# Two places of a form arena filled one block earlier, and its two tiles cut at another form

## The chip, the cores and the metric

The kernel runs on one core of one Trainium2 chip. The metric is the device time of one execution in microseconds (us); lower is better. Times of a kernel are given as the median of several executions. One further execution of each kernel is recorded by the hardware profiler; all rows shown below come from such a profiled execution.

## The reference

One encoder block on x of shape (1, 512, 2048), all in float32: a norm and a combined input projection, two attention mixers, an output projection with a residual, a gated feed-forward network with a residual, and a final norm. The change touches how the feed-forward part's operands are laid out and brought in:

```python
x = x + jnp.einsum('bse,ed->bsd', mixed, w_out[layer])
h2 = rmsnorm(x, g_ffn[layer])
gate, up = jnp.split(jnp.einsum('bsd,df->bsf', h2, w_gate_up[layer]), 2, axis=-1)
x = x + jnp.einsum('bsf,fd->bsd', jax.nn.silu(gate) * up, w_down[layer])
return rmsnorm(x, g_final)
```

Here d = 2048 and f = 5632, so w_down is (5632, 2048): 44 row chunks of 128, taken in 22 pairs.

## The kernel before, in words

**Arithmetic.** Each float32 operand is split in a high part, which ScalarE (ACT) rounds to TensorE's own format, and a low part, which VectorE (DVE) makes by subtraction. A product is three matmuls (`mm3`, lines 231 to 233): high by high, high by low, low by high.

**Seven forms.** Large products go by a scheme of Strassen's kind: for each pair of row chunks, the left operand (activations) is turned into seven *forms* (`m1` to `m7`), sums and differences of its quarters, and so is the weight side. Seven products replace eight.

**The arena.** The left forms lie in an SBUF arena with 7 forms by 8 pairs by (high, low) by 256 columns. It consists of two tiles: `arena[0]` with the first `EARLY` = 3 forms of `ORDER`, `arena[1]` with the other 4. `form_tile(m, pairs)` finds a place by form and pair. The same memory serves other data in earlier stages (`WA_HOMES`, `O_HOMES`, `place`).

**Head.** While the first projection runs, `x_prep(k)` transposes chunk k of x on TensorE, ACT copies it out and makes its high parts (line 327), DVE its low parts (line 328). When both chunks of a pair are there, `x_sums` makes the sums (lines of `form_sums`, 349), and `x_split` splits them: two ACT instructions (line 344) and two DVE instructions (line 345) a pair, each for two neighbouring forms.

**The down projection.** The gate and up blocks write the forms of their result to DRAM (`forms_dram`). The down product runs over its 22 pairs in three groups, `DOWN_PAIRS = (6, 8, 8)`, since the arena holds 8 pairs. Every group is two column blocks (`down_block`, 1024 output columns each), called here block (group, column block). A block goes through the forms in the order `CHAIN` = m1, m7, m6, m2, m5, m4, m3 (with m5 moved in front of most of m2), a unit for each form and pair: 42 units in a block of group 0, 56 in the others. A unit is one weight form split into `tw` (ACT line 755, DVE line 758), for four of the seven forms after a DVE sum or difference of raw weights (line 795), and six matmuls. ACT and DVE prepare a unit some 8 us of planned time ahead.

**Queues.** Raw weights are loaded by SP's queue (`Raw.load`, line 260) 20 us of planned time ahead, as tiles come free. What the blocks add up is evicted by ACT (line 1133) and added into DRAM by POOL's queue (line 1134).

**The next group's forms.** `next_forms(box, first, pairs)` brings the forms of the next group into the arena while the last block of the group before runs, and on into the group's own first block. Each form comes in pieces of up to 4 pairs. A piece is three steps: a load on ACT's DMA queue into one of two `fr` tiles (line 1107), the high part on ACT (line 1110), the low part on DVE (line 1113). The steps hang on unit numbers (`hook`): the form's last unit plus 4 for each form before it, plus 4 for the second piece, and then -5, +1 and +3 for the three steps. Group 0 fills only places 0 to 5 of every form; group 1 fills all 8 places, as two pieces of 4 pairs a form.

**Order of the work.** A loop over all units issues, for each unit in turn, the loads, the splits ahead, the unit's matmuls and then its hooks. Every engine goes through its own instructions in that order, so an instruction that waits holds back all that follow on its engine, the DMA issues on ACT included.

Of the kernel before, what the change touches and what calls it, by code (L numbers as in the profile page):

```python
# [11 lines left out]
F32 = mybir.dt.float32  # L12
BF16 = mybir.dt.bfloat16
F32R = mybir.dt.float32r
AF = mybir.ActivationFunctionType
OP = mybir.AluOpType
# [3 lines left out]
P = 128  # L20
# [4 lines left out]
KD = D // P  # L25
# [25 lines left out]
RAWS = {"raw": 6, "craw": 24, "craw0": 24, "kraw": 9, "craw40": 18, "draw6": 21, "draw8": 28}  # L51
W_TILES = {"wi": 10, "wo": 12}
DOWN_PAIRS = (6, 8, 8)
ORDER = ("m1", "m7", "m6", "m2", "m4", "m5", "m3")
EARLY = 3
EVICT = 6
HEAD_RATE = (1.42, 1.9)
TURN_LAG = 6
# [5 lines left out]
def f32(ap):  # L64
    return ap.bitcast(F32)
# [3 lines left out]
def encoder_block(ctx, tc, x, g_mix, w_in, g_q_a, g_k_a, g_out_a, g_out_b, w_out, g_ffn,  # L69
# [75 lines left out]

    def form_tile(m, pairs):
        return arena[0][:, m, pairs] if m < EARLY else arena[1][:, m - EARLY, pairs]

    def place(m, i):
        return form_tile(m, i).rearrange("p a b -> p (a b)")  # L150
# [78 lines left out]
    def mm3(dst, a, b, start, stop, chained=False):  # L229
        (ah, al), (bh, bl) = a, b  # L230
        nc.tensor.matmul(dst, ah, bh, start=start, stop=False, skip_group_check=chained)  # L231
        nc.tensor.matmul(dst, ah, bl, start=False, stop=False, skip_group_check=chained)  # L232
        nc.tensor.matmul(dst, al, bh, start=False, stop=stop, skip_group_check=chained)  # L233

    def cols(pair, lo, n=P):
        return pair[0][:, lo:lo + n], pair[1][:, lo:lo + n]
# [4 lines left out]
    def in_turn(tiles, n, shape, dtype, tag):  # L241
        if not tiles and homing[0]:
            whole = sp.tile([P, n] + shape[1:], dtype, tag=tag + "s", bufs=1, name=nm(tag))
            tiles.extend(whole[:, i] for i in range(n))
        if not tiles:
            tiles.extend(sp.tile(shape, dtype, tag=tag, bufs=n, name=nm(tag)) for _ in range(n))
        tiles.append(tiles.pop(0))
        return tiles[-1]

    class Raw:  # L250
        def __init__(self, pieces, first=0, tag="raw", width=2 * 512):
            self.pieces, self.first, self.tag, self.width, self.t = pieces, first, tag, width, None
# [11 lines left out]
    class Unit:  # L264
# [22 lines left out]
        def split_lo(self):  # L287
            nc.vector.tensor_tensor(self.w[1], self.src, f32(self.w[0]), op=OP.subtract)  # L288
# [7 lines left out]
    def hook(n, f):  # L296
        hooks.setdefault(n, []).append(f)
# [11 lines left out]
    def x_prep(k):  # L309
        ps = bank()  # L310
        for t in range(NT):
            nc.tensor.transpose(ps[:, t * P:(t + 1) * P], xs[k][:, t, :], ident)
        i, half = divmod(k, 2)
        if half == 0:
            xpair[i] = in_turn(pairs_turn, 3, [P, 4 * 512], F32, "xpair")
        flat = xpair[i][:, half * 1024:half * 1024 + 512]
        view = flat.rearrange("p (f c) -> p f c", c=256)
        hi, lo = (arena[half][:, 0:2, i, j] for j in range(2))
        gain = gm[:, k:k + 1]
        if k == 0:  # L320
            ps3 = ps.rearrange("p (f c) -> p f c", c=256)
            nc.scalar.activation(hi, ps3, AF.Copy, scale=gain)
            nc.vector.scalar_tensor_tensor(lo, ps3, gain, f32(hi), op0=OP.mult, op1=OP.subtract)
            nc.scalar.activation(flat, ps, AF.Copy, scale=gain)
        else:
            nc.scalar.activation(flat, ps, AF.Copy, scale=gain)
            nc.scalar.activation(hi, view, AF.Copy)
            nc.vector.tensor_tensor(lo, view, f32(hi), op=OP.subtract)  # L328
        release(ps)
        row_squares(k)  # L330
        if half == 0:
            hook(k, lambda: nc.gpsimd.dma_start(ar_dram[:, i], arena[0][:, 1, i]))
        else:
            hook(k + 2, lambda: x_sums(i))
            hook(k + 3, lambda: x_split(i))
# [4 lines left out]

    def x_split(i):
        parts = xpair[i].rearrange("p (f c) -> p f c", c=256)
        for src, dst in ((parts[:, 2:4], arena[0][:, 1:3, i]), (parts[:, 6:8], arena[1][:, 2:4, i])):
            nc.scalar.activation(dst[:, :, 0], src, AF.Copy)
            nc.vector.tensor_tensor(dst[:, :, 1], src, f32(dst[:, :, 0]), op=OP.subtract)

    def form_sums(a_l, a_r, b_l, b_r, s1, s2, s3, s4):
        def tt(out, x, y, op=OP.subtract):
# [377 lines left out]
    def form_of(form, i):  # L726
        t = form_tile(ORDER.index(form), i)
        return t[:, 0], t[:, 1]
# [32 lines left out]
            self.box.multiply(self)  # L761

    class ColBlock:
        def __init__(self, w, row, lo, pairs, plan, tag, ready=None, close=None, chain=CHAIN, apart=False):
            self.pairs, self.plan, self.ready, self.close = pairs, plan, ready, close
            self.banks = dict(CHAIN_BANK, m3="x") if apart else CHAIN_BANK
            self.last_of_bank = LAST_OF_BANK + ("m5",) if apart else LAST_OF_BANK
            self.opening = ("m1", "m7", "m2") + (("m3",) if apart else ())
            self.ps, self.at, self.held = {}, {}, []

            def raw(i, j, q):
                at = row + (2 * q + i) * P
                return Raw(lambda t: [(w[0, at:at + P, lo[j]:lo[j] + 512], t)], tag=tag, width=512)
            kinds = {"a": (0, 0), "b": (0, 1), "c": (1, 1), "d": (1, 0), "e": (0, 1), "f": (1, 0), "g": (1, 1)}
            self.raws = [{n: raw(i, j, q) for n, (i, j) in kinds.items()} for q in range(pairs)]
            order = [(form, q) for form in chain for q in range(pairs)]
            if ready is not None:
                rest = order[6:8] + order[8:3 * pairs] + order[3 * pairs + 6:]
                order = order[:6] + order[3 * pairs:3 * pairs + 6] + rest
            if plan is KEPT:  # L780
                at = 3 * pairs + 2
                order[at:at + 2 * pairs - 2] = order[at + pairs - 2:at + 2 * pairs - 2] + order[at:at + pairs - 2]
            for form, q in order:
                self.at[form] = len(units)
                src, dst = plan[form]
                need = src + (dst,) if dst not in src else src
                units.append(Cols(self, form, q, [self.raws[q][n] for n in need]))
                if close is not None and form == CHAIN[-1]:
                    units[-1].dur = COLS_US / 2
# [14 lines left out]
        def multiply(self, u):  # L804
            dst, i = self.bank_of(u.form), u.i
            if self.ready is not None:
                drain_until(lambda: self.ready[i])
            ending = self.close is not None and u.form == "m3"
            if ending:
                self.held.append(u)  # L810
            for t in range(1 if ending else 2):
                mm3(dst[t], cols(form_of(u.form, i), t * P), (u.pair[:, 0], u.pair[:, 1]),
                    u.form in self.opening and i == 0, i == self.pairs - 1, True)
            if ending and i == self.pairs - 1:
                self.close(self)
# [276 lines left out]
    def load_x1(c, rows):  # L1092
        for t in rows:
            x1.setdefault((c, t), slot("x1"))
            nc.gpsimd.dma_start(x1[c, t], x1_dram[c, t])

    def next_forms(box, first, pairs):
        seq = sorted(CHAIN, key=box.at.get)

        def ready(form, h):  # L1100
            m, st = ORDER.index(form), {}
            lo_q, n = 4 * h, min(4, pairs - 4 * h)
            hi, lo = (form_tile(m, slice(lo_q, lo_q + n))[:, :, j] for j in range(2))

            def load():
                st["t"] = in_turn(frs, 2, [P, 4, 256], F32, "fr")[:, :n]
                nc.scalar.dma_start(st["t"], forms_dram[:, m, first + lo_q:first + lo_q + n])  # L1107

            def split_hi():
                nc.scalar.activation(hi, st["t"], AF.Copy)  # L1110

            def split_lo():
                nc.vector.tensor_tensor(lo, st["t"], f32(hi), op=OP.subtract)  # L1113
            late = 4 * seq.index(form) + 4 * h
            box.after(form, late - 5, load)
            box.after(form, late + 1, split_hi)
            box.after(form, late + 3, split_lo)
        for form in seq:
            for h in range(-(-pairs // 4)):
                ready(form, h)  # L1120

    gfin = []
    fin = {}
    def down_block(first, pairs, cb, last):
        box = ColBlock(w_down, 2 * first * P, (cb * 1024, cb * 1024 + 512), pairs, KEPT, f"draw{pairs}",
                       close=finish if last else None)

        def add(form, i, j):
            def go():
# [92 lines left out]
        write_rows(1, 2)  # L1222

    first = 0
    for n in DOWN_PAIRS:
        next_forms(box, first, n)
        for cb in range(2):
            box = down_block(first, n, cb, (first + n, cb) == (NFF // 2, 1))
        first += n

    at = [0.0]
# [135 lines left out]
```

## Time and profile before

| what | value |
|---|---|
| median of 3 runs | 2020.4 us (2019.68 to 2021.6) |
| profiled execution, its own time | 2024.38 us |
| its span in the profile | 2022.6 us |
| TensorE matmuls (PE) busy | 1989.3 us, 98% |
| DVE busy | 1572.3 us, 78% |
| ACT busy | 1113.3 us, 55% |
| moved by DMA | 390.61 MB |

A group's row has the line, the engine, the operation, written and read tiles with their shapes, the count, then busy us and mean ns of one. A row of waits has who waited, for whom, then us in total, times, and the longest. A row of a stretch has its bounds, its length, then each engine's busy us with its count of instructions in brackets, the granted clock of TensorE (PEclk, 1.00 is full speed), the share of the DMA engines, and GB/s.

### The profile page before, as it was taken

To read this page: it belongs to the slowest core of one execution; us is meant where nothing else is said; L and a number is where in the kernel's file an instruction comes from. 1 tells how busy PE (TensorE), PEld (TensorE's weight loads), DVE (VectorE), ACT (ScalarE), POOL (GpSimd) and SP (SyncE) were. 2 spreads that over 40 slices of the span, in tenths; PEclk is the share of its full clock that TensorE was granted. 3 is DMA by queue.
4 is the path that set the end of the run, shared out by engine and by line. 5 is a ranking of instruction groups with operands and counts; after the bars stand their busy time and mean duration, and the time that the engine had idled before them with its cause. 6 is when DMAs were issued, how large, how long until landed. Compare 5 with 4: busy or idle time off the path is not lost. (4 is left out here: it accounts for less than half of the span.)

```text
span 2022.6 us, 27400 instructions
## 1 busy us (share of the span) xinstructions
PE 1989.3 (98%) x9019; PEld 1633.7 (81%) x9019; DVE 1572.3 (78%) x2773; ACT 1113.3 (55%) x1964; POOL 149.9 (7%) x172
## 2 busy tenths in 40 slices
PE   9999999999999999999999999999999999999997
PEld 6788887887788888888888888888888887788886
DVE  7988866576754688878877878878779986887876
ACT  7655345555543565555555555555556665666655
POOL 4100100000010000000000000000000121111122
PEclk9999999999999999999999999999999999999999
DMA  8576533335244545737647657558458798768854
GB/s 267 188 261 228 177 115 103 110 115 171 89 147 140 205 145 198 260 128 259 237 140 273 210 173 273 175 185 287 149 203 280 194 243 256 196 168 261 224 113 178
DMA packets 231391, 390.61 MB, mean 193 GB/s; under 512 B 21408, under 2 KB 70352, under 8 KB 231120
## 3 DMA queue, kind: packets, MB, share of 16 engines
q1 hardware_dynamic: 204880, 326.13, 48.0%
q0 software_dynamic: 14960, 33.04, 8.0%
q10 hardware_dynamic: 11408, 29.70, 4.2%
q8 instruction: 70, 1.15, 0.2%
q14 instruction: 73, 0.60, 0.1%
HBM read 325.08 MB, written 63.70 MB: 192 GB/s over the span
## 5 line engine op out<-in xcount | busy, mean ns | idle before, releaser
L231 PE MATMUL b<-tw,arena 128*128 128x512 f32 x2136 | 838.8, 393 | 4.3 <-ACT ev L1133 2.2
L232 PE MATMUL b<-tw,arena 128*128 128x512 f32 x2136 | 834.4, 391 | 4.2 <-DVE tw L758 3.2
L233 PE MATMUL b<-tw,arena 128*128 128x512 f32 x2136 | 834.1, 390 | 3.4 <-DVE arena L328 3.4
L755 ACT ACTIVATE tw<-raw 128x512 fp32r<-128x512 f32 x924 | 559.5, 628 | 443.7 <-DVE raw L795 286.0
L758 DVE TENSOR_TENSOR tw<-raw,tw 128x512 fp32r<-128x512 f32 x924 | 618.1, 685 | 174.2 <-ACT tw L755 172.1
L232 PEld LDWEIGHTS b<-tw,arena 128*128 128x128 f32 x2136 | 402.1, 188 | 90.5 <-DVE tw L758 7.6
L233 PEld LDWEIGHTS b<-tw,arena 128*128 128x128 f32 x2136 | 401.9, 188 | 89.4 <-DVE arena L328 5.7
L231 PEld LDWEIGHTS b<-tw,arena 128*128 128x128 f32 x2136 | 402.1, 188 | 87.2 <-ACT ev L1133 2.9
L795 DVE TENSOR_TENSOR raw<-raw,raw 128x512 f32<-128x512 f32 x528 | 360.6, 683 | 0.9 <-DMA raw<-in_w_gate_up_dram 0.6
L1134 POOL DMA_DIRECT2D x1d<-ev x76 | 66.5, 978 | 1158.5 <-ACT ev L1133 1157.0
L231 PE MATMUL b<-w,arena 128*128 128x512 f32 x368 | 146.1, 397 | 0.0
L233 PE MATMUL b<-w,arena 128*128 128x512 f32 x368 | 143.8, 391 | 0.0
L232 PE MATMUL b<-w,arena 128*128 128x512 f32 x368 | 143.4, 390 | 0.0
L233 PEld LDWEIGHTS b<-w,arena 128*128 128x128 f32 x368 | 69.1, 188 | 15.0
L232 PEld LDWEIGHTS b<-w,arena 128*128 128x128 f32 x368 | 69.2, 188 | 13.8
L231 PEld LDWEIGHTS b<-w,arena 128*128 128x128 f32 x368 | 69.1, 188 | 13.6
L755 ACT ACTIVATE tw<-stage 128x512 fp32r<-128x512 f32 x90 | 54.5, 628 | 42.2 <-DVE stage L795 33.2
L223 DVE TENSOR_TENSOR pTl<-b,pTh 128x512 fp32r<-128x512 f32 x64 | 44.0, 687 | 34.9 <-ACT pTh L222 24.1
L288 DVE TENSOR_TENSOR w<-raw,w 128x512 fp32r<-128x512 f32 x96 | 64.7, 684 | 5.6 <-ACT w L283 3.2
L349 DVE TENSOR_TENSOR pair<-pair 128x256 f32<-128x256 f32 x120 | 45.5, 420 | 27.3 <-ACT pair L990 26.2
L1133 ACT ACTIVATE ev<-b,smalls 128x512 f32<-128x512 f32 x76 | 49.7, 683 | 26.4 <-PE b L233 25.1
L1037 DVE TENSOR_TENSOR s<-b,s 128x512 f32<-128x512 f32 x66 | 44.0, 687 | 24.8 <-PE b L233 24.8
(197 smaller groups left out, 1808.1 us busy)
## 6 DMA issues: line engine op xcount, KB each, us to landing
raw<-in_w_gate_up_dram SPq DMA_DIRECT2D x616, 256.0 KB, 5.3
raw<-in_w_down_dram SPq DMA_DIRECT2D x176, 256.0 KB, 7.0
stage<-in_w_in_dram SPq DMA_DIRECT2D x106, 256.0 KB, 4.8
forms<-pair SPq DMA_DIRECT2D x22, 896.0 KB, 5.3
x1d<-ev POOLq DMA_DIRECT2D x76, 256.0 KB, 6.6
fr<-forms ACTq DMA_DIRECT2D x35, 512.0 KB, 5.8
raw<-in_w_in_dram SPq DMA_DIRECT2D x64, 256.0 KB, 4.5
raw<-in_w_out_dram SPq DMA_DIRECT2D x32, 512.0 KB, 4.7
```

The lines of the kernel that those rows point to most:

```text
L223: nc.vector.tensor_tensor(lo, src, f32(hi), op=OP.subtract)
L231: nc.tensor.matmul(dst, ah, bh, start=start, stop=False, skip_group_check=chained)
L232: nc.tensor.matmul(dst, ah, bl, start=False, stop=False, skip_group_check=chained)
L233: nc.tensor.matmul(dst, al, bh, start=False, stop=stop, skip_group_check=chained)
L288: nc.vector.tensor_tensor(self.w[1], self.src, f32(self.w[0]), op=OP.subtract)
L349: nc.vector.tensor_tensor(out, x, y, op=op)
L755: nc.scalar.activation(self.pair[:, 0], self.src, AF.Copy)
L758: nc.vector.tensor_tensor(self.pair[:, 1], self.src, f32(self.pair[:, 0]), op=OP.subtract)
L795: nc.vector.tensor_tensor(t[dst], t[src[0]], t[src[1]], op=OP.add if form == "m6" else OP.subtract)
L1037: nc.vector.tensor_tensor(d[:, t], box.bank_of(form)[t], d[:, t], op=OP.add)
L1133: nc.scalar.activation(e, box.bank_of(form)[t], AF.Copy, scale=r2["r"][:, row:row + 1])
L1134: nc.gpsimd.dma_start(x1_dram[2 * cb + j, row], e, accum_op=OP.add)
```

## The change

- `EARLY` goes from 3 to 2: the arena's tiles hold 2 and 5 forms. Where code addresses two neighbouring forms of one pair, a helper `form_pair` finds the tile. In `x_split` the neighbours m7 and m6 (places 1 and 2) now lie in different tiles, so that piece becomes two: three ACT and three DVE instructions a pair where there were two and two.
- The first two pairs of group 1 (pairs 6 and 7 of the 22) are loaded during block (0, 0) into places 6 and 7 of all seven forms, which group 0 does not use. `spare_forms` does it in four pieces: forms 0 and 1, 2 and 3, 4 and 5 (two pairs of two forms each, as large as a piece of 4 pairs), and form 6 alone (half as large). Piece k is loaded after unit 27 + 4k of the block, its high part made 5 units and its low part 7 units later.
- `next_forms` for group 1 then brings only 6 pairs, as a piece of 4 and a piece of 2 a form, at the same units as before.
- In group 1's blocks pair i uses place (i - 2) mod 8 (`turned`), so the two pairs loaded early come first.

```diff
+SPARE_AT = 27
-EARLY = 3
+EARLY = 2
...
+    def form_pair(m, pairs, j):
+        t, lo = (arena[0], m) if m < EARLY else (arena[1], m - EARLY)
+        return t[:, lo:lo + 2, pairs, j]
...
-        hi, lo = (arena[half][:, 0:2, i, j] for j in range(2))
+        hi, lo = (form_pair(3 * half, i, j) for j in range(2))
...
     def x_split(i):
         parts = xpair[i].rearrange("p (f c) -> p f c", c=256)
-        for src, dst in ((parts[:, 2:4], arena[0][:, 1:3, i]), (parts[:, 6:8], arena[1][:, 2:4, i])):
-            nc.scalar.activation(dst[:, :, 0], src, AF.Copy)
-            nc.vector.tensor_tensor(dst[:, :, 1], src, f32(dst[:, :, 0]), op=OP.subtract)
+        pieces = [(parts[:, 2 + n], [form_tile(1 + n, i)[:, j] for j in range(2)]) for n in range(2)]
+        pieces.append((parts[:, 6:8], [form_pair(5, i, j) for j in range(2)]))
+        for src, (hi, lo) in pieces:
+            nc.scalar.activation(hi, src, AF.Copy)
+            nc.vector.tensor_tensor(lo, src, f32(hi), op=OP.subtract)
...
-                mm3(dst[t], cols(form_of(u.form, i), t * P), (u.pair[:, 0], u.pair[:, 1]),
+                mm3(dst[t], cols(form_of(u.form, (i - self.turned) % (KD // 2)), t * P), (u.pair[:, 0], u.pair[:, 1]),
                     u.form in self.opening and i == 0, i == self.pairs - 1, True)
...
+    def form_task(src, parts):
+        st = {}
+
+        def load():
+            st["t"] = in_turn(frs, 2, [P, 4, 256], F32, "fr")[:, :src.shape[1] * (src.shape[2] if len(src.shape) > 3 else 1)]
+            if len(src.shape) > 3:
+                st["t"] = st["t"].rearrange("p (f q) c -> p f q c", f=src.shape[1])
+            nc.scalar.dma_start(st["t"], src)
+
+        def split_hi():
+            nc.scalar.activation(parts[0], st["t"], AF.Copy)
+
+        def split_lo():
+            nc.vector.tensor_tensor(parts[1], st["t"], f32(parts[0]), op=OP.subtract)
+        return load, split_hi, split_lo
+
+    def spare_forms(box, first, lo_q, n):
+        for k, m in enumerate(range(0, 7, 2)):
+            if m + 1 < 7:
+                src = forms_dram[:, m:m + 2, first:first + n]
+                parts = [form_pair(m, slice(lo_q, lo_q + n), j) for j in range(2)]
+            else:
+                src = forms_dram[:, m, first:first + n]
+                parts = [form_tile(m, slice(lo_q, lo_q + n))[:, :, j] for j in range(2)]
+            for late, f in zip((0, 5, 7), form_task(src, parts)):
+                hook(box.at["m1"] + 1 - box.pairs + SPARE_AT + 4 * k + late, f)
...
     first = 0
-    for n in DOWN_PAIRS:
-        next_forms(box, first, n)
+    for g, n in enumerate(DOWN_PAIRS):
+        spare = KD // 2 - DOWN_PAIRS[0] if g == 1 else 0
+        next_forms(box, first + spare, n - spare)
         for cb in range(2):
-            box = down_block(first, n, cb, (first + n, cb) == (NFF // 2, 1))
+            box = down_block(first, n, cb, (first + n, cb) == (NFF // 2, 1), spare)
+            if (g, cb) == (0, 0):
+                spare_forms(box, n, n, KD // 2 - n)
         first += n
```

`next_forms` now makes its three steps through `form_task`, at the same units; `down_block` and `ColBlock` hand `turned` through.

More of the change, by code (lines that the diff above doesn't have):

```diff
@@ L763, in encoder_block, with __init__ @@
     class ColBlock:
-        def __init__(self, w, row, lo, pairs, plan, tag, ready=None, close=None, chain=CHAIN, apart=False):
+        def __init__(self, w, row, lo, pairs, plan, tag, ready=None, close=None, chain=CHAIN, apart=False, turned=0):
             self.pairs, self.plan, self.ready, self.close = pairs, plan, ready, close
+            self.turned = turned
             self.banks = dict(CHAIN_BANK, m3="x") if apart else CHAIN_BANK
@@ L1100, in ready @@
         def ready(form, h):
[L1101 to L1113, printed above, removed]
+            m, lo_q, n = ORDER.index(form), 4 * h, min(4, pairs - 4 * h)
+            parts = [form_tile(m, slice(lo_q, lo_q + n))[:, :, j] for j in range(2)]
+            load, split_hi, split_lo = form_task(forms_dram[:, m, first + lo_q:first + lo_q + n], parts)
             late = 4 * seq.index(form) + 4 * h
@@ L1123, in encoder_block, with down_block @@
     fin = {}
-    def down_block(first, pairs, cb, last):
+    def down_block(first, pairs, cb, last, turned):
         box = ColBlock(w_down, 2 * first * P, (cb * 1024, cb * 1024 + 512), pairs, KEPT, f"draw{pairs}",
-                       close=finish if last else None)
+                       close=finish if last else None, turned=turned)
         def add(form, i, j):
```

## The prediction

> **What bounds the kernel now.** I read the page first: TensorE is busy 98% of the span.
>
> ```profile
> span 2022.6 us, 27400 instructions
> PE 1989.3 (98%) x9019; PEld 1633.7 (81%) x9019; DVE 1572.3 (78%) x2773; ACT 1113.3 (55%) x1964; POOL 149.9 (7%) x172
> ```
>
> Only 33 us are not PE's, so a small change can act in two ways alone: take away a place where PE waits, or make one. The waits of PE over the whole span name four groups that lie in lines the change touches or near them:
>
> ```profile
> PE b L233 <- DVE arena L328: 3.4, 5, 1.1
> PE b L232 <- DVE tw L758: 3.2, 6, 1.6
> PE b L231 <- ACT ev L1133: 2.2, 2, 1.7
> PE b L231 <- ACT tw L755: 2.1, 1, 2.1
> ```
>
> The first group is in the head (20 to 70 us). The other three lie nearly all around the start of block (1, 0), the block whose forms the change brings earlier. The busy time by stretches, three of 44 us, shows what is lost there:
>
> ```profile
> 1652.00:1696.00 44.00, 44.00 (x195) 36.21 (x193) 33.22 (x50) 26.48 (x43) 8.71 (x10) 1.00 0.96 271
> 1696.00:1740.00 44.00, 39.31 (x161) 30.82 (x161) 37.61 (x56) 27.50 (x45) 5.84 (x8) 0.96 0.61 156
> 1740.00:1784.00 44.00, 44.00 (x196) 36.43 (x195) 31.92 (x51) 27.24 (x46) 8.11 (x10) 1.00 0.91 249
> ```
>
> PE starts 161 matmuls in the middle stretch where its neighbours hold 195.5: 34.5 too few, at 44 / 195.5 = 0.225 us each some 7.7 us. That is all that an earlier arrival of forms can win. Who ended it? The timeline of ACT:
>
> ```profile
> 1689.01 0.62 ACT L755 ACTIVATE tw<-raw 128x512 fp32r<-128x512 f32 x1
> 1697.19 0.33 ACTq L1107 DMA_DIRECT2D fr<-forms  x1
> 1697.56 0.63 ACT L755 ACTIVATE tw<-raw 128x512 fp32r<-128x512 f32 x1 [7.92 <-DMA raw<-in_w_down_dram]
> ```
>
> ACT computes nothing for 7.9 us, and the first thing it does afterwards is to issue a load of forms (line 1107); the release is put down to the landing of a weight load. So the form load itself stood in the queue behind a weight load. SP's own waits say that the two queues are coupled so:
>
> ```profile
> SPq L260 <- DMA raw<-in_w_down_dram: 77.6, 73, 7.8
> SPq L260 <- DMA fr<-forms: 26.4, 5, 12.1
> ```
>
> An issue waits for the landing of an earlier transfer, weights for forms too; by the timeline, forms for weights likewise. Only a limited number is under way, and when the transfers are slow, ACT stands still at its issue, with all its splits behind it. PE lived on prepared weights from 1689.6 (end of the last split) to about 1696.1 (2.1 us before it could go on at 1698.2): a cover of 6.5 us. The transfers are slow because two stretches are full:
>
> ```profile
> 1614.00:1636.00 22.00, 22.00 (x99) 18.22 (x98) 17.95 (x30) 14.84 (x25) 5.23 (x6) 1.00 1.06 304
> 1636.00:1661.00 25.00, 25.00 (x112) 20.71 (x111) 20.62 (x33) 15.18 (x25) 5.24 (x6) 1.00 0.85 199
> 1661.00:1698.00 37.00, 35.12 (x155) 28.73 (x154) 24.22 (x36) 20.63 (x34) 6.97 (x8) 1.00 1.04 309
> 1698.00:1702.00 4.00, 3.54 (x8) 2.64 (x9) 3.08 (x5) 2.70 (x5) 0.00 (x0) 0.59 0.83 313
> ```
>
> After the hold, the chain that ended last (asked for 1680 to 1760) runs through DVE and ACT until PE's next long wait ends at 1739; these are its pieces that belong to forms:
>
> ```profile
> 1706.97 1.22 DVE arena L1113
> 1717.14 0.95 ACT arena L1110
> 1719.25 1.22 DVE arena L1113
> 1731.26 1.05 ACT arena L1110
> 1733.47 1.22 DVE arena L1113
> 1739.05 0.50 PE b L231
> ```
>
> ```profile
> L1107 ACTq DMA_DIRECT2D fr<-forms x14: 325/326/327, 1639.1 to 1736.6; - x14
> ```
>
> The 14 form loads of group 1 (tile fr, 1639 to 1740) alternate between first and second piece; the 1.22 us at 1706.97, 1719.25 and 1733.47 are second pieces, and so are both ACT pieces.
>
> **Part by part: group 1's second pieces become half as large.** Prices of whole and half pieces from the rows of tile fr (the least is the half piece):
>
> ```profile
> L1110 ACT ACTIVATE arena<-fr x42: 615/1047/1071, 1514.8 to 1897.1; 128x1024 fp32r<-128x1024 f32 x35, 128x512 fp32r<-128x512 f32 x7
> L1113 DVE TENSOR_TENSOR arena<-fr,arena x42: 680/1216/1221, 1518.3 to 1899.3; 128x1024 fp32r<-128x1024 f32 x35, 128x512 fp32r<-128x512 f32 x7
> fr<-forms ACTq DMA_DIRECT2D x35, 512.0 KB, 5.8
> ```
>
> On the chain: 3 x (1.216 - 0.680) = 1.6 us of DVE and 2 x (1.047 - 0.615) = 0.9 us of ACT, together 2.5 us. Before the hold ends, one second piece (the one of m6) is loaded wholly within the full stretch; its 256 KB less are 262 KB / 309 GB/s = 0.85 us, by which the weight load that ACT waits for lands sooner. A second one (m7's) overlaps the stretch's beginning: at most 1.7 us for both. Against it, DVE's backlog from the new pieces could start the stretch later. I take 0.8. Sum of this part: -3.3 us; bounds 0 (the later start eats it, and the chain is replaced by the next) and -7.7 (everything regained).
>
> The clock: in the 4 us after the 2.1 us stall the granted clock is 0.59, worth 4 x 0.41 = 1.6 us. I count nothing for it, because the chain behind it is DVE's and ACT's: a faster PE would reach its next wait sooner. If that cover is thinner than I think, the forecast is 1.6 us lower. The Trainium skill, "TensorE: Matmul & The Clock Gate", Part 1, has the clock halved after an idle window of about 3.4 us; by it a 2.1 us stall should cost no clock and a shorter one could give none back, so the sum stays; the 0.59 disagrees with it, and leaves the 1.6 us open.
>
> **The four new pieces in block (0, 0).** They add three whole loads and a half one, 3.5 x 512 KB = 1.84 MB, from about 1618 us on, in a stretch that moves 304 GB/s at a DMA share of 1.06: 1.84 / 304 is 6.0 us of transfers pushed back, into 1636 to 1661 with its 199 GB/s. "DMA: Bandwidth & Descriptors", section "Issuing engines are not separate DMA queues" of the Trainium skill says the same of ACT's queue: another issuer brings no other engines, so nothing of the 6.0 us hides by being ACT's; here the share of 1.06 agrees. ACT gets 3 x 1.05 + 0.62 = 3.8 us more, DVE 3 x 1.22 + 0.68 = 4.3 us. DVE is idle 22 - 17.95 = 4.1 us before 1636 and 4.4 us in the next 25; it fits, barely. ACT has room:
>
> ```profile
> ACT ev L1133 <- PE b L233: 5.5, 2, 2.8
> ```
>
> and SP's queue, from which the new loads take their turns, holds
>
> ```profile
> 1614.69 21.06 SPq L260 DMA_DIRECT2D raw<-in_w_down_dram  x21
> ```
>
> The row of ACT is of its waits from 1615 to 1641. The four issues are 0.33 us each. The third load stands behind the eviction of m4 on ACT, which waits for PE; behind the fourth stand the splits of block (0, 1). I expect holds of 2 to 4 us there, within the cover of 6.5: cost 0, with an upper bound of 3.7 us (below). A gain here is excluded: PE has no wait from 1614 to 1661.
>
> **The head.** `x_split` makes two DVE instructions of 256 columns out of one of 512, for 8 pairs:
>
> ```profile
> 40.00:47.00 7.00, 6.43 (x32) 5.21 (x32) 6.97 (x10) 5.72 (x10) 3.11 (x4) 1.00 0.59 177
> 54.00:61.00 7.00, 6.39 (x31) 4.90 (x29) 6.96 (x11) 5.69 (x11) 3.11 (x4) 1.00 0.31 87
> L345 DVE TENSOR_TENSOR arena<-xpair,arena 128x512 fp32r<-128x512 f32 x16 | 10.3, 681 | 0.3 <-ACT arena L344 0.3
> L349 DVE TENSOR_TENSOR pair<-pair 128x256 f32<-128x256 f32 x120 | 45.5, 420 | 27.3 <-ACT pair L990 26.2
> L349 DVE TENSOR_TENSOR xpair<-xpair 128x256 f32<-128x256 f32 x32 | 18.5, 618 | 0.3
> ```
>
> DVE is full there (6.97 of 7 us), and PE waits for it five times. An instruction of 256 columns takes 0.420 us, or 0.618 us where POOL works beside it: 2 x 0.420 - 0.681 = +0.16 us a pair, or +0.56. Line 345 at 0.681 is not one of the slowed ones, so I take 0.16. For the five pairs at which PE waits +0.8 us; bounds 0.8 and 8 x 0.56 = 4.4 us. ACT's extra piece is hidden: ACT is idle 1.3 us of 7. The other uses of the arena (`h_side`, the places of weights and attention outputs) keep their number of instructions and elements: 0, and no PE wait covers them.
>
> **Sum.** -3.3 + 0.8 + 0 = -2.5 us: the profiled execution's 2024.4 (span 2022.6 plus 1.8 around it) becomes 2021.9. The median lies 4.0 us under the profiled execution: 2020.4 - 2.5 = 2017.9.
>
> **Rivals.** *All of it goes.* If the hold gets shorter by the 1.7 us of both pieces, PE's first wait nearly vanishes, the clock stays up, and the chain starts ahead of PE instead of behind it: -7.7 + 0.8 = -6.9, 2013.5. For it: hold and cover differ by little more than 1.4 us. Against it: DVE has 37.6 of 44 us of work in that stretch with or without the hold.
>
> *Slower: the hold moves.* The new loads stand in the other full stretch (304 GB/s), among 21 weight loads. If one of them waits as long as the one at 1697, 7.9 us, the same cover of 6.5 us breaks: 2.1 us of stall and 1.6 us of clock at the end of block (0, 0). DVE, with all its idle time spent, then starts the next full stretch late, so nothing is regained in block (1, 0): +3.7 + 0.8 = +4.5, 2024.9. It decides from the point where ACT's gap before a spare load's issue exceeds 6.5 us. For it: the 6.0 us of pushed transfers; against it: ACT's 5.5 us of waiting for PE, and the loads come early in their stretch, the one at 1697 at the end of its own. By the clock rule named above it would be 1.6 us less, 2023.3.
>
> *It does not act.* If the weights, not the forms, set the hold, nothing changes in block (1, 0), and the head remains: 2021.2.
>
> **How the numbers follow.** 0.2% is 4 us, about what a measurement of this kernel can tell from no change. The forecast of a small gain has 0.33, not acting 0.07, everything regained (or most of it, with the clock's 1.6 us) 0.35, the moved hold or a costly head 0.25. The first lies within 0.2% but for its lowest end, not acting within it: faster 0.36, same 0.39, slower 0.25. The range takes in full recovery and most of the moved hold: 2013.3 to 2024.6. The forecast's own range is 2015 to 2020.
>
> **What would show it.** In the changed profile: line 1113 with 7 more half pieces in 1639 to 1745; ACT's gap before the split that opens block (1, 0) at 6.5 to 7 us instead of 7.9; PE's matmuls in those 44 us near 176; the five waits on line 328 longer by 0.16 each. Wrong would be: a PE wait between 1630 and 1661, a granted clock under 1 there, ACT's gap unchanged, or the waits on line 328 grown by over 2 us in sum.

## The result, and the profile after

| kernel | median, us | before in the same runs, us | ratio to before, 95% interval |
|---|---|---|---|
| after | 2027.89 | 2020.85 | 1.0035 (1.0025 to 1.0045) |

The change made the kernel 0.35% slower, about 7.1 us (5.1 to 9.1). Forecast were 2017.9 us, 2.5 us less than before, in a range that ended at 2024.6. The profiled execution has an own time of 2027.2 us. The page's first lines, of the kernel after:

```profile
span 2025.4 us, 27426 instructions
PE 1990.8 (98%) x9019; PEld 1630.6 (81%) x9019; DVE 1573.8 (78%) x2785; ACT 1113.6 (55%) x1976; POOL 152.8 (8%) x172
```

The shares are what they were; again only waits of PE can hold the difference. The busy time by stretches, of the kernel after:

```profile
1616.00:1662.00 46.00, 43.64 (x182) 33.25 (x181) 32.27 (x49) 25.60 (x42) 8.71 (x10) 1.00 0.91 256
1652.00:1696.00 44.00, 42.94 (x188) 34.84 (x187) 39.38 (x63) 29.31 (x50) 8.73 (x10) 1.00 0.90 232
1696.00:1740.00 44.00, 43.50 (x188) 34.71 (x187) 35.59 (x56) 26.55 (x45) 6.98 (x8) 1.00 0.72 183
1698.00:1702.00 4.00, 4.00 (x19) 3.34 (x18) 0.69 (x1) 0.44 (x1) 1.50 (x2) 1.00 1.05 390
```

and the stretch of block (0, 0) in the kernel before:

```profile
1616.00:1662.00 46.00, 46.00 (x205) 38.09 (x204) 37.57 (x60) 29.95 (x50) 10.47 (x12) 1.00 0.94 249
```

Two things happened. Around the start of block (1, 0) the change worked: 188 matmuls start in 1696 to 1740 where 161 did (172 in a second profile of the kernel before, shown below), and the stall with the low clock at 1698 is gone. But in the stretch in which the new pieces are brought in, 1616 to 1662, PE starts 182 matmuls where it started 205: 23 fewer, at 46 / 205 = 0.224 us each 5.2 us. Matmul by matmul, the kernel after falls 6.8 us behind the one before between 1632 and 1668 and wins back 4.7 us by 1739.

ACT's timeline in that stretch, kernel after, shows where it was lost:

```profile
1620.72 0.38 ACTq L1112 DMA_DIRECT2D fr<-forms  x1
...
1624.78 1.15 ACT L762 ACTIVATE tw<-raw 128x512 fp32r<-128x512 f32 x2
1631.81 0.37 ACTq L1112 DMA_DIRECT2D fr<-forms  x1
1632.22 0.63 ACT L762 ACTIVATE tw<-raw 128x512 fp32r<-128x512 f32 x1 [6.29 <-DMA fr<-forms]
...
1638.39 0.37 ACTq L1112 DMA_DIRECT2D fr<-forms  x1
1638.81 0.63 ACT L762 ACTIVATE tw<-raw 128x512 fp32r<-128x512 f32 x1 [2.29 <-DMA raw<-in_w_down_dram]
...
1646.76 1.06 ACT L1115 ACTIVATE arena<-fr 128x1024 fp32r<-128x1024 f32 x1 [2.84 <-DMA fr<-forms]
```

The first new load is issued at 1620.72. The rows of tile fr for 1618 to 1624 give its time to the landing:

```profile
L1112 ACTq DMA_DIRECT2D fr<-forms x1: 380/380/380, 1620.7 to 1620.7; - x1
DMA to landing us min/median/max: 11.0/11.0/11.0
```

It landed 11.0 us later, at 1631.7, and only then, at 1631.81, could ACT issue the second one; the splits of weights stood behind that issue for 6.29 us. What the issue waits for stands in the trace's records of the instructions. Every transfer counts up a semaphore when it lands; the transfers of SP and ACT share eight of them, taken in turn in the program's order, and those of GpSimd have eight others. ACT's instruction ahead of the second new load waits for the very semaphore that the first one counts up, whose last count came at 1631.71. For six of the eight every count can be put down to its transfer, and of 912 such issues in this trace none came before the transfer that had the same semaphore last had landed. So at most eight transfers of SP and ACT together are under way, by waits that the compiled program holds; whether the queues have a limit of their own is not shown.

The following holds came before any lead had been built up again. ACT's waits for transfers in 1614 to 1662, kernel after:

```profile
ACT tw L762 <- DMA fr<-forms: 6.3, 1, 6.3
...
ACT tw L762 <- DMA raw<-in_w_down_dram: 3.6, 2, 2.3
ACT arena L1115 <- DMA fr<-forms: 3.1, 2, 2.8
```

Together 13.0 us; the kernel before had 0.3 us of them. The lead is read from DVE's last split before the hold and PE's first wait behind it (kernel after, timelines of DVE and of PE's weight loads):

```profile
1625.45 1.30 DVE L765 TENSOR_TENSOR tw<-raw,tw 128x512 fp32r<-128x512 f32 x2
...
1639.47 0.69 DVE L765 TENSOR_TENSOR tw<-raw,tw 128x512 fp32r<-128x512 f32 x1 [2.09 <-ACT tw L762]
...
1648.37 0.69 DVE L765 TENSOR_TENSOR tw<-raw,tw 128x512 fp32r<-128x512 f32 x1 [3.73 <-ACT tw L762]
```

```profile
1632.90 0.19 PEld L236 LDWEIGHTS b<-tw,arena 128*128 128x128 f32 x1 [0.47 <-ACT tw L762]
```

The split ends at 1626.75 and PE has run dry at 1632.90 - 0.47 = 1632.43: a cover of 5.7 us. Counted as the prediction counted it, from the end of ACT's last split (1624.78 + 1.15 = 1625.93), it is 6.5 us, the very number that the prediction took. 13.0 of holds less 5.7 or 6.5 of cover is 7.3 or 6.5 us, near the 6.8 that PE lost. Between the holds ACT works only 4.3, 3.1 and 0.6 us before it stands again, and DVE waits for it (the 2.09 and 3.73 us above), so the cover is there once. Most of what PE lost shows at its weight loads, not at its matmuls; the waits of PEld in 1614 to 1662, kernel after:

```profile
PEld b L237 <- DVE tw L765: 4.2, 8, 1.1
PEld b L236 <- ACT tw L762: 1.9, 3, 1.2
```

### The profile page after: what moved, and what is told of

Read it like the earlier page. It is cut to its first block, busy times and chain, and to the rows that moved or that the text cites. A ratio compares the mean times of both kernels' runs of the same rounds, so it can differ in the third digit from the quotient of the medians.

```text
span 2025.4 us, 27426 instructions
## 1 busy us (share of the span) xinstructions
PE 1990.8 (98%) x9019; PEld 1630.6 (81%) x9019; DVE 1573.8 (78%) x2785; ACT 1113.6 (55%) x1976; POOL 152.8 (8%) x172
## 3 DMA queue, kind: packets, MB, share of 16 engines
q8 instruction: 70, 1.15, 0.2%
## 5 line engine op out<-in xcount | busy, mean ns | idle before, releaser
L227 ACT ACTIVATE pTh<-b 128x512 fp32r<-128x512 f32 x64 | 37.9, 593 | 45.8 <-PE b L583 40.7
```

The costliest lines, as they stand in the source:

```text
L227: nc.scalar.activation(hi, src, AF.Copy)
```

## The experiments

Line numbers differ between the kernels: the splits of weights on ACT are line 755 before and 761 to 763 in the others, the splits of forms 1110 before and 1115 to 1122. All ratios are to the kernel before, measured beside it on the same chip. The overview; "ACT held" is the sum of ACT's waits for transfers in 1614 to 1662:

| run | median, us | ratio, 95% interval | ACT held, us | matmuls 1616 to 1662 | 1696 to 1740 |
|---|---|---|---|---|---|
| before, profiled again | 2020.2 | 0.9999 (0.9990 to 1.0008) | 0.3 | 205 | 172 |
| after | 2027.89 | 1.0035 (1.0025 to 1.0045) | 13.0 | 182 | 188 |
| tiles only | 2021.56 | 1.0004 (0.9995 to 1.0013) | 0.9 | 204 | 175 |
| new loads on GpSimd's queue | 2027.69 | 1.0031 (1.0019 to 1.0043) | 12.4 | 183 | 173 |
| work without loads | 2016.78 | 0.9981 (0.9972 to 0.9990) | 0 | 205 | 193 |
| loads without splits | 2021.91 | 1.0007 (0.9998 to 1.0016) | 6.1 | 203 | 181 |
| loads early, in place | 2018.65 | 0.9990 (0.9982 to 0.9999) | 1.1 | 205 | 189 |
| loads early, old tiles | 2018.25 | 0.9989 (0.9980 to 0.9998) | 0 | 205 | 190 |
| before, forms on GpSimd's queue | 2019.63 | 0.9999 (0.9990 to 1.0007) | 0.8 | 205 | 178 |
| splits later | 2029.05 | 1.0043 (1.0026 to 1.0060) | 15.4 | 179 | 183 |
| splits later, GpSimd's queue | 2021.6 | 1.0007 (0.9997 to 1.0016) | 1.4 | 205 | 173 |

### The kernel before, profiled again

No edit.

> The kernel before, unchanged, profiled once more. The first profile of it lay 3.5 us above its median and lost 7.7 us of PE in 1696 to 1740 us with a granted clock of 0.59 for a while. Theory 'lucky and unlucky executions': the usual execution loses less there (about 4 us, 178 matmuls in those 44 us instead of 161, no low clock), and the time is 2021 as before. Rival 'the loss is always there': 161 to 165 matmuls again and a profiled time near the first one.

The rows of the second profile, its stretch and the ACT split that opens block (1, 0):

```profile
1696.00:1740.00 44.00, 40.77 (x172) 31.86 (x173) 39.65 (x59) 28.19 (x45) 6.96 (x8) 1.00 0.64 160
```

```profile
1694.60 1.15 ACT L755 ACTIVATE tw<-raw 128x512 fp32r<-128x512 f32 x2 [5.98 <-DMA raw<-in_w_down_dram]
```

The hold is 5.98 us here and was 7.92 in the profile that the prediction used; 172 matmuls stand for 161, and there is no low clock at 1698, as the first theory said, though more was lost than its 4 us. So the 7.7 us to be won there were those of an execution with a long hold; in this one it is (195.5 - 172) x 0.225 = 5.3 us.

### The tiles alone

```diff
-        spare = KD // 2 - DOWN_PAIRS[0] if g == 1 else 0
+        spare = 0
...
-            if (g, cb) == (0, 0):
-                spare_forms(box, n, n, KD // 2 - n)
```

> Only the cut of the arena in tiles of 2 and 5 forms, with the third piece in x_split; no early forms. Theory 'hold' (the change is slower because a spare load holds ACT up in block (0, 0)): the cut costs what the traces show up to 721 us, 0.6 us, so 2021.5. Rival 'tiles' (the cut itself costs the time, in the head or by other waits): 2026 to 2028. Rival 'work' (the early forms' ACT and DVE instructions cost it): 2021.5 as well.

1.0004, or +0.8 us with an interval from -1.0 to +2.6: the forecast's +0.8 for the head fits, and so does nothing. The five waits of PE on the head's low parts, which should have grown by 0.16 us each from 3.4, are these with the tiles alone and in the kernel after:

```profile
PE b L238 <- DVE arena L333: 2.9, 5, 1.1
PE b L238 <- DVE arena L333: 2.5, 5, 0.7
```

They did not grow. At the opening of block (1, 0) this kernel, which brings no form early, has an ACT gap of only 4.21 us:

```profile
1694.36 1.15 ACT L762 ACTIVATE tw<-raw 128x512 fp32r<-128x512 f32 x2 [4.21 <-DMA raw<-in_w_down_dram]
```

With 7.92 and 5.98 in the two profiles of the kernel before, that gap scatters by some 4 us without any early form.

### The new loads on another queue

```diff
-            nc.scalar.dma_start(st["t"], src)
+            (eng or nc.scalar).dma_start(st["t"], src)
...
-            for late, f in zip((0, 5, 7), form_task(src, parts)):
+            for late, f in zip((0, 5, 7), form_task(src, parts, nc.gpsimd)):
```

> The changed kernel, with the four spare loads issued by POOL's queue instead of ACT's; the same bytes, the same units, the same splits. Theory 'hold': ACT no longer stands at an issue between 1620 and 1645, PE keeps 200 or more matmuls in 1616 to 1662 (182 in the changed kernel, 205 before), and block (1, 0) keeps its gain: 2018 to 2021. Rival 'work' and rival 'bytes' (the 1.84 MB delay the weights): PE's loss there stays, 2026 to 2028. Rival 'tiles': 2026 to 2028.

The time stayed. Issued by GpSimd, the loads no longer hold ACT at their issue, but ACT comes to their splits before they have landed (ACT's timeline, and its waits in 1614 to 1662):

```profile
1630.34 1.06 ACT L1115 ACTIVATE arena<-fr 128x1024 fp32r<-128x1024 f32 x1 [4.72 <-DMA fr<-forms]
...
1637.87 1.06 ACT L1115 ACTIVATE arena<-fr 128x1024 fp32r<-128x1024 f32 x1 [3.24 <-DMA fr<-forms]
...
1644.94 1.06 ACT L1115 ACTIVATE arena<-fr 128x1024 fp32r<-128x1024 f32 x1 [3.93 <-DMA fr<-forms]
```

```profile
ACT arena L1115 <- DMA fr<-forms: 12.4, 4, 4.7
```

The hold moved from the issue to the split, with nearly the same sum, 12.4 for 13.0. The first of them lands no sooner, 10.5 us after its issue (11.0 from ACT's queue). This agrees with what the prediction cited from the Trainium skill, "DMA: Bandwidth & Descriptors", "Issuing engines are not separate DMA queues": another issuer brings no other engines.

### The work without the loads, and the loads without the work

Without loads, the splits of the new pieces read neighbouring places of the arena:

```diff
+            if stand_in is not None:
+                st["t"] = stand_in
+                return
...
+                near = f32(form_pair(m, slice(0, n), 0))
...
-            for late, f in zip((0, 5, 7), form_task(src, parts)):
+            for late, f in zip((0, 5, 7), form_task(src, parts, near)):
```

> The changed kernel without the four spare loads: ACT and DVE split, at the same units, what lies in places 0 and 1 of the same forms instead, so the two early pairs hold other numbers than the reference's. Theory 'hold' and rival 'bytes': no loss in 1616 to 1662, the gain in block (1, 0) stays: 2017 to 2020. Rival 'work': 2026 to 2028.

Its stretches:

```profile
1616.00:1662.00 46.00, 46.00 (x205) 38.09 (x204) 41.63 (x64) 32.11 (x54) 10.43 (x12) 1.00 0.94 244
1696.00:1740.00 44.00, 43.63 (x193) 35.81 (x192) 40.73 (x63) 28.05 (x47) 6.96 (x8) 1.00 0.66 154
```

The 4.1 us that DVE works more in the first stretch (41.63 for 37.57) cost PE nothing, and block (1, 0) runs nearly full. With free loads the change is worth 0.9981, or -3.8 us; the loads cost the rest, 1.0035 - 0.9981, about 11 us.

The counterpart has the loads on GpSimd's queue and no splits:

```diff
-            for late, f in zip((0, 5, 7), form_task(src, parts)):
+            for late, f in zip((0,), form_task(src, parts, nc.gpsimd)):
```

> The four spare loads on POOL's queue at the changed kernel's units, and nothing that reads them: the splits are left out, so places 6 and 7 hold old numbers in group 1. No engine waits for the landing. Theory 'late landing': no ACT wait for forms, PE keeps 203 to 205 matmuls in 1616 to 1662, 2017 to 2019. Rival 'bytes' (the weights of block (0, 1) come late by the 6 us of pushed transfers): ACT and DVE wait for weights there, 2023 to 2027.

1.0007, between the two forecasts: the bytes in the full stretch do not by themselves make the 7 us. ACT was held 6.1 us there, about one cover, and PE starts 203 matmuls. But neither is anything gained, although group 1's second pieces are half as large here too. ACT's longest wait for a transfer moved to the first form load of group 1 (waits in 1614 to 1696):

```profile
ACT tw L762 <- DMA fr<-forms: 5.5, 1, 5.5
```

### The loads made early

If late landing is the cause, a load at units 1, 4, 7 and 10 of block (0, 0), ahead of the full stretch, should cost nothing. As the two fr tiles are in use there, it goes straight into the low places, and the low part is made in place; the splits stay at their units.

```diff
+LOAD_AT = 1
...
+            if in_place:
+                st["t"] = f32(parts[1])
+                pairs = [(st["t"], src)] if len(src.shape) == 3 else [(st["t"][:, f], src[:, f]) for f in range(2)]
+                for dst, one in pairs:
+                    nc.scalar.dma_start(dst, one)
+                return
...
+            hook(start + LOAD_AT + 3 * k, load)
+            hook(start + SPARE_AT + 4 * k + 5, split_hi)
+            hook(start + SPARE_AT + 4 * k + 7, split_lo)
```

> The changed kernel, with the spare loads taken out of the full stretch: ACT's queue issues them from unit 1 of block (0, 0) on (about 1581 to 1595 us, where 111 GB/s move), straight into the low parts' places, so no fr tile is needed; the splits stay at the changed kernel's units and make the low part in place. Theory 'late landing' (the loads land 7 to 11 us after their issue in a full stretch, and ACT, which goes through its instructions in order, waits for them at the next issue or at the split): no ACT wait and no PE loss in 1616 to 1662 (205 matmuls), the gain in block (1, 0) stays: 2016 to 2018, like the kernel that did the work without the loads (2016.8). Rival 'bytes' (1.84 MB more cost their time wherever they move in the block): 2024 to 2028.

Its stretches, and its issues in 1578 to 1600:

```profile
1616.00:1662.00 46.00, 46.00 (x205) 38.09 (x204) 41.65 (x65) 33.19 (x55) 10.44 (x12) 1.00 0.96 249
1696.00:1740.00 44.00, 42.90 (x189) 34.82 (x188) 40.70 (x63) 28.07 (x47) 6.97 (x8) 1.00 0.64 150
```

```profile
arena<-forms ACTq DMA_DIRECT2D x7, 256.0 KB, 3.1
```

There the kernel before moves 120 GB/s:

```profile
1578.00:1600.00 22.00, 22.00 (x102) 18.19 (x102) 20.84 (x34) 12.03 (x21) 3.25 (x4) 1.00 0.47 120
```

PE loses nothing in block (0, 0), keeps the gain in block (1, 0), and the kernel beats both others, if by little: 0.9990 (0.9982 to 0.9999). The 2018.65 us lie a little above the forecast 2016 to 2018. The same with the tiles of before (pieces of forms 0 and 1; 2; 3 and 4; 5 and 6, so that no piece lies in both tiles):

```diff
-EARLY = 2
+EARLY = 3
...
-        for k, m in enumerate(range(0, 7, 2)):
-            if m + 1 < 7:
+        for k, (m, two) in enumerate(((0, True), (2, False), (3, True), (5, True))):
+            if two:
```

> The same early loads into place, with the arena's old tiles of 3 and 4 forms and the old x_split; the four pieces are forms 0 and 1, 2, 3 and 4, 5 and 6. Theory 'late landing' with a small cost of the tile cut: 0.5 to 1.2 us under the kernel with the new tiles, 2015 to 2017. Theory that the tile cut is free: the same time. Rival 'bytes': 2023 to 2028.

0.9989: the new cut of the arena is not needed, and its cost is too small to be told from none.

### The forms of before on GpSimd's queue

```diff
-                nc.scalar.dma_start(st["t"], forms_dram[:, m, first + lo_q:first + lo_q + n])
+                (nc.gpsimd if first else nc.scalar).dma_start(st["t"], forms_dram[:, m, first + lo_q:first + lo_q + n])
```

> The kernel before, with the form loads of groups 1 and 2 issued by POOL's queue; no early forms. Theory 'hold at the issue' (what costs PE 4 to 8 us at the start of block (1, 0) is ACT standing at the issue of a form load): the gap of 7.9 us on ACT is gone and PE keeps 190 or more matmuls in 1696 to 1740 (161 and 172 in the two profiles of the kernel before): 2015 to 2017. Theory 'late landing': the wait moves from the issue to the split of the same form and the time stays, 2019 to 2022.

0.9999, with 178 matmuls where the first theory had 190 or more: the second one holds. The hold at the opening of block (1, 0), too, moves from the issue to the split (ACT's timeline):

```profile
1692.76 1.06 ACT L1110 ACTIVATE arena<-fr 128x1024 fp32r<-128x1024 f32 x1 [3.01 <-DMA fr<-forms]
```

### The splits made later

Left open was which of two waits it takes: for the landing of the first load at the second one's issue, or for the landing at the split. Both kernels load at the units of the kernel after (27, 31, 35, 39), in place, and split 8 units later than it; the second one also issues from GpSimd.

```diff
+LOAD_AT = 27
...
+            hook(start + LOAD_AT + 4 * k, load)
+            hook(start + SPARE_AT + 4 * k + 13, split_hi)
+            hook(start + SPARE_AT + 4 * k + 15, split_lo)
```

```diff
-                    nc.scalar.dma_start(dst, one)
+                    nc.gpsimd.dma_start(dst, one)
```

> The kernel after, with its early loads issued by ACT at the same units of block (0, 0) as there (27, 31, 35, 39) but straight into the low places, and the two splits of each piece 8 units (some 11 us) later than there: 13 and 15 units after the load. Theory 'late landing' (a load of 512 KB takes 7 to 11 us in the full stretch, its split comes 6.8 us after the issue): the waits of ACT and DVE for the landing go, but the second load can still stand behind the first one at its issue (6.3 us in the kernel after); so between 2018.5 and 2023 us, by whether that hold stays. Rival 'bytes in the full stretch' (the transfers of the early loads push back the weights, whenever the splits come): stays at 2026 to 2028 us. Rival 'work of ACT and DVE': no less than 2026 us.

> The same as the splits made 8 units later, with the early loads issued by GpSimd's queue, so that ACT neither issues them nor meets them before they have landed. 'Late landing': no hold of ACT between 1614 and 1662 us is left, PE starts 203 to 205 matmuls in 1616 to 1662 (182 in the kernel after), the gain in block (1, 0) stays: 2018 to 2020 us, like the loads made early. 'Bytes in the full stretch': 2026 to 2028 us.

The first came out slowest of all, 1.0043, above every range that was named for it; late landing had been given at most 2023 us, with the hold at the issue included, so its price was missed. (That the engines' work would give no less than 2026 fits the number, but the work without loads has excluded it; the bytes' 2026 to 2028 is near, but the second kernel moves the same bytes.) Late splits alone are no help, since ACT is now held at the issues of the second, third and fourth piece, 4.8, 4.5 and 4.2 us (the first two in its timeline below; seven loads of 256 KB take more of the eight turns than four of 512 KB):

```profile
1627.71 1.90 ACTq L1114 DMA_DIRECT2D arena<-forms  x2
1629.65 2.20 ACT L763 ACTIVATE tw<-raw 128x512 fp32r<-128x512 f32 x4 [4.76 <-DMA raw<-in_w_down_dram]
1635.94 1.46 ACTq L1114 DMA_DIRECT2D arena<-forms  x2
1637.45 2.19 ACT L763 ACTIVATE tw<-raw 128x512 fp32r<-128x512 f32 x4 [4.45 <-DMA arena<-forms]
```

In the second, neither wait is left: ACT is held 1.4 us, PE starts all 205 matmuls of 1616 to 1662, and the slowdown is gone (1.0007). Its code differs from the first kernel's only in the queue that issues the seven loads, which is worth 0.36%, or 7.3 us: what counts here is which engine stands at the issue. The time is a little above the expected 2018 to 2020, since the gain in block (1, 0) went with it:

```profile
1616.00:1662.00 46.00, 46.00 (x205) 38.10 (x204) 37.51 (x58) 30.66 (x51) 15.81 (x19) 1.00 0.97 266
1696.00:1740.00 44.00, 41.27 (x173) 33.15 (x172) 37.44 (x59) 28.04 (x47) 6.87 (x8) 0.96 0.63 153
```

```profile
1698.34 1.15 ACT L763 ACTIVATE tw<-raw 128x512 fp32r<-128x512 f32 x2 [6.43 <-DMA raw<-in_w_down_dram]
```

## Why the prediction was wrong, step by step

**The step that failed** is, in the part on the four new pieces in block (0, 0), "I expect holds of 2 to 4 us there, within the cover of 6.5: cost 0, with an upper bound of 3.7 us". The holds were 6.3, 3.6 and 3.1 us, in sum 13.0, against one cover of 5.7 to 6.5, and PE lost 6.8 us. The prediction's own sign of being wrong, a PE wait between 1630 and 1661, is there (2.1 us at its matmuls in 1614 to 1662). Two errors are in it. One is of size: the step took its pushed-back 6.0 us as a matter of throughput and never asked when a load issued in a stretch of 304 GB/s lands. The median of 5.8 us that it quoted is of all stretches; here it was 11.0, so the second issue waited for the first load. The other is of kind: it held each hold against the whole cover. Four pieces follow each other every 4 units, and ACT and DVE rebuild no lead between them, so the holds add up.

**The rival "the hold moves"** had the mechanism and the sign, but not the price: it put the decision at a single gap over 6.5 us, and the largest was 6.29. It decides by the sum of the holds. It was also wrong that nothing would then be regained in block (1, 0).

**Smaller second pieces** were sized about right: -4.7 us against the first profile and -2.9 against the second, for a forecast of -3.3, and with the loads free the whole change is worth -3.8 us where -2.5 was forecast. Matmul by matmul against the second profile, 2.7 of the 2.9 us come between 1704 and 1739, on the chain behind the hold, for which 2.5 were forecast; there the work without loads wins 4.3 us and the tiles alone 0.4. The 0.8 us for a shorter hold are not shown: ACT's gap is 4.59 us here, less than the 6.5 to 7 foreseen, but with the tiles alone it was 4.21. The seven half pieces and one more at the window's end are there (kernel after; opening split, then tile fr in 1648 to 1760):

```profile
1703.03 1.15 ACT L762 ACTIVATE tw<-raw 128x512 fp32r<-128x512 f32 x2 [4.59 <-DMA raw<-in_w_down_dram]
```

```profile
L1118 DVE TENSOR_TENSOR arena<-fr,arena x16: 681/952/1222, 1649.0 to 1750.4; 128x1024 fp32r<-128x1024 f32 x8, 128x512 fp32r<-128x512 f32 x8
```

**The engines' extra work** (3.8 us of ACT, 4.3 us of DVE, "it fits, barely") was right, as the work without loads shows. **The head's 0.8 us** stays open: the interval of the tiles alone holds it and zero.

**Where the 11 us of the loads go**, by differences of ratios: from the kernel after to late splits on GpSimd's queue, where ACT's holds are gone, 0.28% or 5.7 us; from there to the loads made early, 0.17% or 3.4 us; the remaining 0.09%, 1.8 us, is within the intervals. The second difference fits the bytes pushed from the full stretch towards the next one (ACT's gap at the opening of block (1, 0) is 6.43 with them and 4.75 without), but that gap scatters as much by itself (4.21 to 7.92), and these two kernels also differ in when they split and in the queue, so this share is argued, not shown.

**The median** was taken 4.0 us under the profiled execution, as the prediction said; that execution had a longer hold than the second one, and a gain read from it was partly chance: matmul by matmul, 1.8 of the 4.5 us between the two are lost at the opening of block (1, 0).

## What to carry to other kernels

Before bringing a load forward into idle memory, look at how full the transfers are at the new place, and take the time from issue to landing there, not the median of all. On an engine that works in order, add up the holds of loads that follow each other closely, at the issue and at the first use, and compare their sum with the lead once: moving only one of the two waits moves the hold. Look, too, at which earlier load an issue waits for: here SP's and ACT's queues share eight semaphores, so it was the transfer that held the same one before. The same loads 40 us earlier, where the queues were half empty, turned a loss of 0.35% into a gain of 0.1%.

## What was not expected of the hardware

A 512 KB load took 11.0 us to land where 298 GB/s were moved (1618 to 1632, kernel after). 256 KB took a median of 3.1 us where, with these loads, 184 GB/s were moved (1578 to 1600, loads early), and 8.4 us where 314 GB/s were (1616 to 1645, splits later):

```profile
arena<-forms ACTq DMA_DIRECT2D x7, 256.0 KB, 8.4
```

The granted clock did not go by the length of a stall alone. In the first profile of before a stall of 2.1 us was followed by a low clock (0.59 in the 4 us from 1698), and in the kernel with late splits on GpSimd's queue one of 2.0 us:

```profile
PE b L237 <- ACT tw L763: 2.0, 1, 2.0
```

```profile
1698.00:1702.00 4.00, 2.75 (x6) 2.01 (x7) 2.30 (x4) 3.14 (x5) 0.00 (x0) 0.72 1.04 344
```

In the kernel before with its forms on GpSimd's queue a stall of 1.71 us, up to 1733.04, was enough; in the second profile of before one of 1.68 us, up to 1736.09, was not. The clock records of the traces tell them apart. A low clock lasts 3.41 us or twice that (but for the last of a trace), and within a trace the low clocks begin whole multiples of 3.41 us apart. On that beat the stall of 1.71 us lies within one period and leaves PE 1.71 us of work there, and the one of 1.68 us is cut in two (each pair of rows is one period and the next):

```profile
1730.00:1733.41 3.41, 1.71 (x7) 1.10 (x8) 3.41 (x7) 2.26 (x5) 0.00 (x0) 1.00 0.61 193
1733.41:1736.82 3.41, 3.41 (x10) 2.64 (x9) 3.20 (x6) 2.73 (x5) 1.79 (x2) 0.50 0.75 175
```

```profile
1731.79:1735.20 3.41, 2.50 (x10) 1.42 (x8) 3.41 (x6) 1.64 (x3) 0.00 (x0) 1.00 0.21 30
1735.20:1738.61 3.41, 2.52 (x11) 2.10 (x12) 3.24 (x6) 3.41 (x7) 1.73 (x2) 1.00 0.91 302
```

Counted so over all twelve traces, from 100 us on to shortly before PE's last matmul, PE was busy 0.98 to 1.77 us in the period ahead of each of 23 falls, and 1.74 us or more in every period that no fall followed (the ends of matmuls are modelled): about half of 3.41 us divides them. The Trainium skill, "TensorE: Matmul & The Clock Gate", Part 1, as the prediction cited it, has the clock halved after an idle window of about 3.4 us; the length of the window agrees with these traces, but a wholly idle one was not needed.
